# Retention queries and keys of a four-branch decoder trunk: projected and rotated feature-major, with only the keys transposed

## The chip, the cores and the metric

The kernel runs on one core of one Trainium2 chip. The metric is the device time of one execution in microseconds; a kernel's time is the median of its runs.

## What is computed

A trunk of two layers on 1024 tokens of width 1024. Each layer normalises its input, modulates it, and projects it through one input matrix to the inputs of four mixing branches (HGRN2, retention, Mamba-2 SSD, GLA). The branch outputs are normed per head, gated and projected back. The change concerns the retention branch, four heads of width 128:

```python
def rotary(t):
    ...
    t1, t2 = tf[..., : d // 2], tf[..., d // 2:]
    return jnp.concatenate([t1 * cos - t2 * sin, t1 * sin + t2 * cos], axis=-1)

def retention_branch(q_in, k_in, v_in, g_in, onorm_g):
    q = rotary(to_heads(q_in, RET_HEADS))
    k = rotary(to_heads(k_in, RET_HEADS)) * (dk ** -0.5)
    ...
    o = chunked_scalar_decay(q, k, to_heads(v_in, RET_HEADS), log_a)
    return group_rmsnorm(from_heads(o), onorm_g, RET_HEADS) * jax.nn.silu(g_in)
```

The chunked sum is, per chunk of 128 tokens here: scores of queries against keys times a decay mask, times the values, plus the queries times a carried state; the state takes up decayed keys times values.

## The kernel before

**Operands.** All large matmuls run in fp32r with both operands split into a high part (a cast) and a low part (the rest), as three matmuls: high by high, high by low, low by high. The normalised input lies feature-major in SBUF (`hh`, `hl`: 8 k-tiles of 128 features by 1024 tokens, in two halves of 512 tokens). Weights come in slices of 128 x 512 on SP's queue (`raw`, two buffers); ScalarE casts the high part (L405) and VectorE subtracts for the low part (L406), into four buffers each.

**Two forms of the input projection.** `proj_f` (L424) makes 128 output features for all 1024 tokens: the weights stand still in the array and 512 tokens pass, 16 steps of three matmuls of 512 columns (L420 to L422), results feature-major in two PSUM banks. `proj_t` (L453) makes 256 output features for all tokens: 128 tokens stand still and 256 weight columns pass, 64 steps of three matmuls of 256 columns (L467, L469, L470), results token-major in four PSUM banks. All projections share a pool of four banks (`pp`). Both call an `evac` function as each bank is finished.

**The order of work.** The order on TensorE is the order in which the program is written, and it is interleaved by hand. A mixing function is a generator that yields the nanoseconds of other work wanted at that point. `run` hands them to `fill`, which takes steps from a queue of projection generators, each step with a price of its own: 640 for a `proj_f` step or for half an output unit (three matmuls of 512 columns), 320 for a `proj_t` step. `drain(p)` takes the rest of the queue up to generator p. On the other engines and the DMA queues a scheduler orders the instructions, and each queue runs in order.

**The retention stage.** While the second SSD group is mixed (`ssd_mix`, L1029), the queue holds an output projection, then `ret_qk` for head 0 (L865) and `vg_proj` for its values and gates. While head h is mixed (`ret_mix`, L890) the queue holds `ret_qk` and `vg_proj` for head h + 1, for head 0 behind the output projection of tiles 10 and 11. For head 3 it holds the output projection of tiles 4 and 5 (16 units of two steps), then that of tiles 6 and 7 (`out_tiles`, L1173), whose weights are loaded, multiplied by the gate on GpSimd (L1148) and split when it starts.

`ret_qk` projects query and key of one head together with `proj_t`. For each bank (two token tiles) ScalarE copies queries and keys to SBUF (L877), VectorE makes four products per query and key with the cosine and sine tables (L881 to L884), and GpSimd subtracts and adds them (L885, L886). `ret_mix` then transposes eight query and eight key tiles on TensorE (L897), copies them out on ScalarE (L898), scales the token-major keys by the decay to the chunk's end on VectorE (L900), yields 1200, makes the scores (L910) and their mask product (L912), and goes through `scan` (L652): scores by values (L661), keys by values (L667, into bank `ms`), queries by state (L671), the state update (L677), and the head norm with its gate (`head_norm_gate`: squares L541 on ScalarE, rsqrt L272 and L274 on GpSimd, the product L545 on VectorE). The normed output is transposed (L524) some steps later.

Large tiles of 128 x 1024 (tables, queries, keys, values, gates and others) share eleven buffers, tiles of 128 x 512 five. In the SSD mix TensorE writes each chunk's output to bank `po` (L1102), which VectorE reads (L1117, L1120).

Of the kernel before, what the change touches and what calls it, by code (L numbers as in the profile page):

```python
# [16 lines left out]
AF = mybir.ActivationFunctionType  # L17
ALU = mybir.AluOpType
MUL, ADD, SUB = ALU.mult, ALU.add, ALU.subtract
PSUM = bass.MemoryType.PSUM  # L20

P = 128
# [3 lines left out]
NT = L // P  # L26
DEPTH = 2
EPS = 1e-6
C = 128
NC = L // C  # L30
# [5 lines left out]
RQ, RK, RV, RG = 2048, 2560, 3072, 3584  # L36
# [9 lines left out]
def _f(name, col):  # L46
    F_UNITS[name] = len(F_COLS)
    F_COLS.append(col)


def _t(name, c0, c1):
    T_UNITS[name] = len(T_COLS)
    T_COLS.append((c0, c1))
# [15 lines left out]
    _f(("mc", _g), MX + 768 + 128 * _g)  # L69
    _t(("mz", _g), MZ + 256 * _g, MZ + 256 * _g + 128)  # L70
for _h in range(4):
    _t(("rqk", _h), RQ + 128 * _h, RK + 128 * _h)
    _t(("rvg", _h), RV + 128 * _h, RG + 128 * _h)


# [38 lines left out]
CST, NCST = {}, 0  # L114
# [16 lines left out]
def shape_constants():  # L131
    i = np.arange(P)
    out = np.zeros((P, NCST), np.float64)

    def put(name, a):
        o, n = CST[name]
        out[:, o : o + n] = np.asarray(a).reshape(P, n)

    put("ident", np.eye(P))
    put("upper", i[:, None] <= i[None, :])  # L140
    put("ones", np.ones((P, P)))
    log_gamma = np.log1p(-np.exp2(-(5.0 + np.arange(4))))
    dk = 128.0 ** -0.5
    causal = (i[:, None] <= i[None, :]).astype(np.float64)
    grow = np.exp(-log_gamma[None, :] * (i[:, None] + 1))
    put("rmask", causal[:, None, :] * grow[:, :, None] * dk)
    put("rke", np.exp(log_gamma[None, :] * (C - 1 - i[:, None])) * dk)
    put("reps", EPS * grow * grow)
    inv_freq = (10000.0 ** (-np.arange(0, 128, 2, dtype=np.float32) / np.float32(128))).astype(np.float32)
    ang = np.arange(L, dtype=np.float32)[:, None] * inv_freq[None, :]  # L150
    ang = ang.reshape(NT, P, 64).transpose(1, 0, 2).astype(np.float64)
    rot = np.stack([np.cos(ang), np.sin(ang)], axis=1).reshape(P, 2 * NT * 64)
    return out.astype(np.float32), rot.astype(np.float32), [float(np.exp(g * C)) for g in log_gamma]


# [11 lines left out]
def hybrid_trunk(ctx, nc, tc, t_in, out, gamma_c):  # L167
    vec, act, gp, pe = nc.vector, nc.scalar, nc.gpsimd, nc.tensor
# [14 lines left out]
    def nm(s):  # L183
        seq[0] += 1
        return f"{s}_{seq[0]}"

    def big_t():
        return big.tile([P, 1024], F32, tag="b4", name=nm("b4"))

    def mid_t(n=512):  # L190
        return mid.tile([P, 512], F32, tag="b2", name=nm("b2"))[:, :n]
# [4 lines left out]
    def ps_proj():  # L196
        return pp.tile([P, 512], F32, tag="pp", name=nm("pp"))

    def ps_mix(tag, bufs=1):
        return pm.tile([P, 512], F32, tag=tag, bufs=bufs, name=nm(tag))  # L200
# [34 lines left out]
    cs = cst.tile([P, NCST], F32, name="cs")  # L235
# [5 lines left out]
    def k_(name, sub=None):  # L241
        o, n = CST[name]
        return cs[:, o : o + n]
# [5 lines left out]
    ident, upper, ones = k_("ident"), k_("upper"), k_("ones")  # L249
# [27 lines left out]
    def bc(ap, shape):  # L277
        return ap.to_broadcast(shape)
# [145 lines left out]
    def proj_f(l, name, evac):  # L424

        pss = [ps_proj(), ps_proj()]
        for k in range(KT):
            if k % 4 == 0:
                w = load_f(l, name, k // 4)
            for half in range(2):  # L430
                step_f(w, pss[half], half, k)
                if k == KT - 1:
                    evac(half, pss[half])
                yield 640
# [18 lines left out]
    def proj_t(l, name, evac):  # L453

        src = t_in["wt"][l, T_UNITS[name]]
        pss = [ps_proj() for _ in range(4)]
        for s in range(4):
            raw = raw_t(512)
            nc.sync.dma_start(raw, src[:, s * 512 : (s + 1) * 512])
            hi, lo = split(raw, 512)  # L460
            for k in (2 * s, 2 * s + 1):
                j = (k % 2) * 256
                for m in range(NT):
                    o = pss[m // 2][:, (m % 2) * 256 : (m % 2) * 256 + 256]
                    hhi = hh[m // 4][:, k, (m % 4) * P : (m % 4) * P + P]
                    hlo = hl[m // 4][:, k, (m % 4) * P : (m % 4) * P + P]
                    pe.matmul(o, hhi, hi[:, j : j + 256], start=(k == 0 and m % 2 == 0), stop=False,  # L467
                              skip_group_check=True)
                    pe.matmul(o, hhi, lo[:, j : j + 256], start=False, stop=False, skip_group_check=True)  # L469
                    pe.matmul(o, hlo, hi[:, j : j + 256], start=False, stop=(k == KT - 1), skip_group_check=True)  # L470
                    if k == KT - 1 and m % 2:
                        evac(m // 2, pss[m // 2].rearrange("p (m c) -> p m c", m=2))
                    yield 320
# [255 lines left out]
    def vg_tiles():  # L729
        return (big_t().rearrange("p (m c) -> p m c", m=NT), big_t().rearrange("p (m c) -> p m c", m=NT))  # L730
# [127 lines left out]


    def ret_tables():  # L860
        rt = big_t()
        nc.sync.dma_start(rt, t_in["rot"])
        return (rt[:, 0:512].rearrange("p (m d) -> p m d", m=NT), rt[:, 512:1024].rearrange("p (m d) -> p m d", m=NT))

    def ret_qk(l, h, tables, u):  # L865
        if not tables:
            tables.extend(ret_tables())
        cos, sin = tables

        def ev(j, ps):  # L870
            if j == 0:
                u["q"], u["k"] = vg_tiles()
            ms_ = slice(2 * j, 2 * j + 2)
            c2 = cos[:, ms_, :]
            s2 = sin[:, ms_, :]
            for qk, o in (("q", 0), ("k", 128)):
                act.copy(u[qk][:, ms_, :], ps[:, :, o : o + 128])  # L877
            for qk in ("q", "k"):
                x1, x2 = u[qk][:, ms_, 0:64], u[qk][:, ms_, 64:128]
                t = mid_t().rearrange("p (i m d) -> p i m d", i=4, m=2)  # L880
                vec.tensor_tensor(t[:, 0], x1, c2, MUL)  # L881
                vec.tensor_tensor(t[:, 1], x2, s2, MUL)
                vec.tensor_tensor(t[:, 2], x1, s2, MUL)
                vec.tensor_tensor(t[:, 3], x2, c2, MUL)  # L884
                gp.tensor_tensor(u[qk][:, ms_, 0:64], t[:, 0], t[:, 1], SUB)  # L885
                gp.tensor_tensor(u[qk][:, ms_, 64:128], t[:, 2], t[:, 3], ADD)  # L886

        yield from proj_t(l, ("rqk", h), ev)

    def ret_mix(l, h, u, between=None):  # L890
        AT = ATs[h % 2]
        QT, KTt = big_t(), big_t()
        for half in range(2):
            for src, dst, tag in ((u["q"], QT, "sc"), (u["k"], KTt, ("ms", "po")[half])):
                ps = ps_mix(tag, 2 if tag == "sc" else 1)
                for i in range(4):
                    pe.transpose(ps[:, i * P : (i + 1) * P], src[:, half * 4 + i, :], ident)  # L897
                act.copy(dst[:, half * 512 : half * 512 + 512], ps)  # L898
        o, _ = CST["rke"]
        vec.tensor_scalar(u["k"], u["k"], cs[:, o + h : o + h + 1], None, MUL)  # L900
        ke = u["k"]
        o, _ = CST["rmask"]
        rm = cs[:, o + h * P : o + (h + 1) * P]
        oe, _ = CST["reps"]
        yield 1200
        for half in range(2):
            ps = ps_mix("sc", 2)
            for i in range(4):
                c = half * 4 + i
                pe.matmul(ps[:, i * P : (i + 1) * P], KTt[:, c * C : (c + 1) * C], QT[:, c * C : (c + 1) * C],  # L910
                          start=True, stop=True)
            vec.tensor_tensor(AT[:, half * 4 : half * 4 + 4, :], ps.rearrange("p (c t) -> p c t", c=4),  # L912
                              bc(rm.unsqueeze(1), [P, 4, P]), MUL)
            yield 200
        yield 600
        yield from scan(l, 4 + h, AT, lambda c: QT[:, c * C : (c + 1) * C], lambda c: ke[:, c, :], u["v"], u["g"],
                        lambda c: gamma_c[h], cs[:, oe + h : oe + h + 1], h >= 2, between)
# [324 lines left out]
    u, w0, acc, known = {}, {}, {}, [0, 0]  # L1242
# [75 lines left out]
    for l in range(DEPTH):  # L1318
# [5 lines left out]
        p = add(wide)  # L1324
# [7 lines left out]
        for h in range(4):  # L1332
# [7 lines left out]
            if h < 3:  # L1340
                p = add(hgrn_proj(l, h + 1, nu))
            else:
                p = add(gla_qk(l, 0, nu))
# [12 lines left out]
            u = nu  # L1356
# [8 lines left out]
        for p in range(2):  # L1365
# [16 lines left out]
            u = nu  # L1382
# [4 lines left out]
        for g in range(2):  # L1387
# [4 lines left out]
            if g == 0:  # L1392
                add_out(l, (14, 15))
                p = add(ssd_bc(l, 1, nu))
            else:
# [3 lines left out]
                p = add(vg_proj(l, ("rvg", 0), nu))  # L1399
            run(ssd_mix(l, g, u, st, lambda: more_x(nu) if g == 0 else None))  # L1400
            drain(p)
            u = nu
        for h in range(3):
# [4 lines left out]
            p = add(vg_proj(l, ("rvg", h + 1), nu))  # L1408
            run(ret_mix(l, h, u))
            drain(p)  # L1410
            u = nu
# [19 lines left out]
        if more:  # L1431
            u = {}
# [69 lines left out]
```

## Time and profile before

| what | value |
|---|---|
| median of three runs | 2083.54 us (2083.15 to 2085.19) |
| the profiled execution | 2084.53 us |
| its span, first to last instruction | 2082.7 us |
| TensorE clock granted, mean | 0.993 |
| matmuls | 17994 |
| DMA, mean | 60 GB/s |

The page gives the busy time of each engine (PE is TensorE, PEld its weight loads, DVE VectorE, ACT ScalarE, POOL GpSimd, SP the queue that issues most loads), then the span in slices, the chain of work that ended last, and the costliest groups of instructions: line, engine and operation, output and inputs by the program's names, shape, count, busy time, mean nanoseconds of one, and the idle time just before them with what ended it. Matmuls are pipelined, and their ends in the records are modelled. A row of a timeline has the start in us, the busy time, and the instruction. A row of waits has who waited for whom, the us in total, the times, and the longest. A row of a table by windows has the stretch, then the busy time and count on PE, PEld, DVE, ACT and POOL, the granted clock, and the DMA share and GB/s.

### The profile page before, as it was taken

How to read it: one execution, taken by the hardware profiler on the slowest of the kernel's cores; microseconds unless marked ns; L12 is line 12 of the kernel's file. 1: busy time of each engine (PE TensorE's matmuls, PEld its weight loads, DVE VectorE, ACT ScalarE, POOL GpSimd, SP SyncE). 2: the span in 40 equal slices, each digit the busy share in tenths (PEclk: the TensorE clock that was granted, in tenths of full speed). 3: DMA queues.
4: the chain of work that ended last, by engine and by line, in shares of the span. 5: the costliest groups of instructions: out<-in, count | busy, mean ns of one | idle time of the engine just before them, and what ended most of it. 6: DMA issues, size and time to landing. Idle time of an engine off the chain costs nothing.

```text
span 2082.7 us, 42807 instructions
## 1 busy us (share of the span) xinstructions
PE 2030.5 (97%) x17994; PEld 1822.1 (87%) x17994; DVE 1167.2 (56%) x2347; ACT 757.9 (36%) x1760; POOL 382.6 (18%) x564
## 2 busy tenths in 40 slices
PE   5999999999999999999999999999999999999997
PEld 4898888789888899999879888888988989999996
DVE  7656743836537476444555555356464565744456
ACT  7432223432345343122273223343234444322223
POOL 4101001000123233222220010010101323402232
PEclk9999999999999999999999999999999999999999
DMA  8233321111121120111112211111111212111112
GB/s 283 88 104 97 98 77 32 35 39 37 36 66 57 44 89 26 52 37 31 46 54 71 79 32 42 39 35 38 37 40 37 80 43 72 56 37 42 42 36 101
DMA packets 72304, 124.15 MB, mean 60 GB/s; under 512 B 10128, under 2 KB 20656, under 8 KB 72112
## 3 DMA queue, kind: packets, MB, share of 16 engines
q1 hardware_dynamic: 67216, 112.31, 17.6%
q10 hardware_dynamic: 4896, 9.12, 1.4%
q8 instruction: 141, 2.31, 0.5%
q14 instruction: 51, 0.42, 0.1%
HBM read 117.14 MB, written 4.26 MB: 58 GB/s over the span
## 4 chain that ended last, share of the span: by engine, by line
PE 85%; DVE 7%; ACT 4%; DMA 2%; issue 1%; POOL 1%; SPq 0%; POOLq 0%; ACTq 0%; DVEq 0%
PE pp L1159 14%; PE pp L467 12%; PE pp L469 11%; PE pp L470 11%; PE pp L420 7%; PE pp L422 6%; PE pp L421 6%; DMA wa<-in_w_ada 2%; PE sc L584 2%; PE sc L524 1%; DVE b L612 1%; PE po L1102 1%; PE ms L667 1%; PE pp L502 1%; DVE b L301 1%
## 5 line engine op out<-in xcount | busy, mean ns | idle before, releaser
L467 PE MATMUL pp<-whi,hh 128*128 128x256 f32 x2176 | 631.6, 290 | 0.7 <-ACT b L991 0.7
L469 PE MATMUL pp<-wlo,hh 128*128 128x256 f32 x2176 | 615.9, 283 | 0.0
L470 PE MATMUL pp<-whi,hl 128*128 128x256 f32 x2176 | 615.9, 283 | 0.0
L467 PEld LDWEIGHTS pp<-whi,hh 128*128 128x128 f32 x2176 | 417.2, 192 | 4.7 <-ACT b L991 1.5
L469 PEld LDWEIGHTS pp<-wlo,hh 128*128 128x128 f32 x2176 | 417.6, 192 | 0.5
L470 PEld LDWEIGHTS pp<-whi,hl 128*128 128x128 f32 x2176 | 417.1, 192 | 0.0
L405 ACT CAST whi<-raw 128x512 fp32r<-128x512 f32 x280 | 173.6, 623 | 593.9 <-PE pp L470 296.3
L406 DVE TENSOR_TENSOR wlo<-raw,whi 128x512 fp32r<-128x512 f32 x276 | 200.1, 729 | 282.2 <-ACT whi L405 275.2
L420 PE MATMUL pp<-hh,whi 128*128 128x512 f32 x640 | 268.2, 419 | 7.4 <-ACT hh L397 6.6
L422 PE MATMUL pp<-hl,whi 128*128 128x512 f32 x640 | 252.6, 395 | 1.4 <-DVE hl L398 1.3
L421 PE MATMUL pp<-hh,wlo 128*128 128x512 f32 x640 | 251.0, 392 | 0.0
L1164 DVE TENSOR_TENSOR xs<-xs,pp 128x512 f32<-128x512 f32 x256 | 172.9, 684 | 70.8 <-PE pp L1159 68.1
L1159 PE MATMUL pp<-whi,yh 128*128 128x512 f32 x448 | 188.4, 420 | 0.0
L1148 POOL TENSOR_TENSOR raw<-raw,gate_b 128x512 f32<-128x512 f32 x64 | 84.6, 1325 | 521.2 <-DMA raw<-in_w_out 407.3
L1159 PE MATMUL pp<-whi,yl 128*128 128x512 f32 x448 | 175.5, 392 | 0.0
L1159 PE MATMUL pp<-wlo,yh 128*128 128x512 f32 x448 | 174.9, 390 | 0.0
L420 PEld LDWEIGHTS pp<-hh,whi 128*128 128x128 f32 x640 | 120.9, 189 | 32.9 <-ACT hh L397 8.6
L422 PEld LDWEIGHTS pp<-hl,whi 128*128 128x128 f32 x640 | 120.6, 188 | 32.3 <-DVE hl L398 5.5
L421 PEld LDWEIGHTS pp<-hh,wlo 128*128 128x128 f32 x640 | 121.3, 190 | 20.1 <-DVE wlo L406 0.4
L272 POOL TENSOR_SCALAR rt<-ss 128x4 f32<-128x4 f32 (+1 forms) x46 | 12.2, 265 | 556.6 <-ACT junk L541 498.2
L301 DVE SCALAR_TENSOR_TENSOR b<-wa,c_act,b 128x512 f32<-128x512 f32 x84 | 71.2, 847 | 61.7 <-DMA wa<-in_w_ada 60.9
L1159 PEld LDWEIGHTS pp<-whi,yh 128*128 128x128 f32 x448 | 84.4, 188 | 21.1 <-issue 3.4
(257 smaller groups left out, 3075.4 us busy)
## 6 DMA issues: line engine op xcount, KB each, us to landing
raw<-in_wt SPq DMA_DIRECT2D x136, 256.0 KB, 3.0
wa<-in_w_ada SPq DMA_DIRECT2D x96, 256.0 KB, 2.9
raw<-in_wf SPq DMA_DIRECT2D x80, 256.0 KB, 2.6
raw<-in_w_out SPq DMA_DIRECT2D x64, 256.0 KB, 2.6
b<-cum ACTq DMA_DIRECT2D x32, 256.0 KB, 3.5
xs<-in_x SPq DMA_DIRECT2D x8, 512.0 KB, 8.1
out<-b SPq DMA_DIRECT2D x7, 512.0 KB, 2.6
b<-in_wt SPq DMA_DIRECT2D x4, 384.0 KB, 4.1
```

The source lines that it names most:

```text
L301: vec.scalar_tensor_tensor(acc, w, c_act[:, k : k + 1], acc, MUL, ADD)
L405: act.copy(hi, raw)
L406: eng.tensor_tensor(lo, raw, hi.bitcast(F32), SUB)
L420: pe.matmul(ps, hi[:, j : j + P], hh[half][:, k, :], start=(k == 0), stop=False)
L421: pe.matmul(ps, lo[:, j : j + P], hh[half][:, k, :], start=False, stop=False)
L422: pe.matmul(ps, hi[:, j : j + P], hl[half][:, k, :], start=False, stop=(k == KT - 1))
L467: pe.matmul(o, hhi, hi[:, j : j + 256], start=(k == 0 and m % 2 == 0), stop=False, skip_group_check=True)
L469: pe.matmul(o, hhi, lo[:, j : j + 256], start=False, stop=False, skip_group_check=True)
L470: pe.matmul(o, hlo, hi[:, j : j + 256], start=False, stop=(k == KT - 1), skip_group_check=True)
L1148: gp.tensor_tensor(raw, raw, gate_b[:, nh * 512 : (nh + 1) * 512], MUL)
L1159: pe.matmul(ps, a[:, o : o + P], b, start=(n == 0), stop=(n == 3 * len(kts) - 1))
L1164: vec.tensor_tensor(xv, xv, ps, ADD)
```

## The change

The units `rqk` of `proj_t` are replaced by two units of `proj_f` a head, one for the queries and one for the keys. The two tables are laid out feature-major, 128 x 1024 each, the sine with its sign. Of each finished bank ScalarE copies the two halves of 64 features crosswise to SBUF, VectorE multiplies the bank by the cosine, and GpSimd multiplies the crossed copy by the sine and adds it. The mix uses queries and keys as they come; it transposes only the keys, and ScalarE applies the scale of the keys while it copies them out. The `yield 1200` behind the transposes is gone.

```diff
 for _h in range(4):
-    _t(("rqk", _h), RQ + 128 * _h, RK + 128 * _h)
+    _f(("rq", _h), RQ + 128 * _h)
+    _f(("rk", _h), RK + 128 * _h)
     _t(("rvg", _h), RV + 128 * _h, RG + 128 * _h)
...
-    ang = ang.reshape(NT, P, 64).transpose(1, 0, 2).astype(np.float64)
-    rot = np.stack([np.cos(ang), np.sin(ang)], axis=1).reshape(P, 2 * NT * 64)
+    ang = ang.T.astype(np.float64)
+    cos, sin = np.cos(ang), np.sin(ang)
+    rot = np.stack([np.concatenate([cos, cos]), np.concatenate([-sin, sin])])
...
     def ret_tables():
-        rt = big_t()
-        nc.sync.dma_start(rt, t_in["rot"])
-        return (rt[:, 0:512].rearrange("p (m d) -> p m d", m=NT), rt[:, 512:1024].rearrange("p (m d) -> p m d", m=NT))
+        rt = [big_t(), big_t()]
+        for i in range(2):
+            nc.sync.dma_start(rt[i], t_in["rot"][i])
+        return rt
...
-        def ev(j, ps):
-            if j == 0:
-                u["q"], u["k"] = vg_tiles()
-            ms_ = slice(2 * j, 2 * j + 2)
-            c2 = cos[:, ms_, :]
-            s2 = sin[:, ms_, :]
-            for qk, o in (("q", 0), ("k", 128)):
-                act.copy(u[qk][:, ms_, :], ps[:, :, o : o + 128])
-            for qk in ("q", "k"):
-                x1, x2 = u[qk][:, ms_, 0:64], u[qk][:, ms_, 64:128]
-                t = mid_t().rearrange("p (i m d) -> p i m d", i=4, m=2)
-                vec.tensor_tensor(t[:, 0], x1, c2, MUL)
-                vec.tensor_tensor(t[:, 1], x2, s2, MUL)
-                vec.tensor_tensor(t[:, 2], x1, s2, MUL)
-                vec.tensor_tensor(t[:, 3], x2, c2, MUL)
-                gp.tensor_tensor(u[qk][:, ms_, 0:64], t[:, 0], t[:, 1], SUB)
-                gp.tensor_tensor(u[qk][:, ms_, 64:128], t[:, 2], t[:, 3], ADD)
-
-        yield from proj_t(l, ("rqk", h), ev)
+        def ev(name):
+            def ev_(half, ps):
+                if half == 0:
+                    u[name] = big_t()
+                s = slice(half * 512, half * 512 + 512)
+                t = mid_t()
+                act.copy(t[0:64, :], ps[64:P, :])
+                act.copy(t[64:P, :], ps[0:64, :])
+                vec.tensor_tensor(u[name][:, s], ps, cos[:, s], MUL)
+                gp.tensor_tensor(t, t, sin[:, s], MUL)
+                gp.tensor_tensor(u[name][:, s], u[name][:, s], t, ADD)
+            return ev_
+
+        yield from proj_f(l, ("rq", h), ev("q"))
+        yield from proj_f(l, ("rk", h), ev("k"))
...
-        QT, KTt = big_t(), big_t()
+        QT, KTt = u["q"], u["k"]
+        o, _ = CST["rke"]
+        ke = big_t().rearrange("p (c d) -> p c d", c=NC)
         for half in range(2):
-            for src, dst, tag in ((u["q"], QT, "sc"), (u["k"], KTt, ("ms", "po")[half])):
-                ps = ps_mix(tag, 2 if tag == "sc" else 1)
-                for i in range(4):
-                    pe.transpose(ps[:, i * P : (i + 1) * P], src[:, half * 4 + i, :], ident)
-                act.copy(dst[:, half * 512 : half * 512 + 512], ps)
-        o, _ = CST["rke"]
-        vec.tensor_scalar(u["k"], u["k"], cs[:, o + h : o + h + 1], None, MUL)
-        ke = u["k"]
+            ps = ps_mix(("ms", "po")[half])
+            for i in range(4):
+                c = half * 4 + i
+                pe.transpose(ps[:, i * P : (i + 1) * P], KTt[:, c * C : (c + 1) * C], ident)
+            act.activation(ke[:, half * 4 : half * 4 + 4, :], ps.rearrange("p (c d) -> p c d", c=4), AF.Copy,
+                           scale=cs[:, o + h : o + h + 1])
...
-        yield 1200
```

## The prediction

> **What bounds the kernel now.** I read the page's busy table and granted clock first, then the chain that ended last.
>
> ```profile
> span 2082.7 us, 42807 instructions
> PE 2030.5 (97%) x17994; PEld 1822.1 (87%) x17994; DVE 1167.2 (56%) x2347; ACT 757.9 (36%) x1760; POOL 382.6 (18%) x564
> PE 85%; DVE 7%; ACT 4%; DMA 2%; issue 1%; POOL 1%; SPq 0%; POOLq 0%; ACTq 0%; DVEq 0%
> L467 PE MATMUL pp<-whi,hh 128*128 128x256 f32 x2176 | 631.6, 290 | 0.7 <-ACT b L991 0.7
> ```
>
> TensorE carries the kernel: what leaves its instruction stream leaves the time, as long as the other engines stay ahead of it. The column "mean ns of one" is a trap here: matmuls overlap, so 290 ns is a life, not a spacing. The price of a matmul is the distance between starts, and that is in the timeline of TensorE. First a stretch of a token-major projection, then one of a feature-major projection:
>
> ```profile
> 719.72 0.28 PE L470 MATMUL pp<-whi,hl 128*128 128x256 f32 x1
> ...
> 725.84 0.28 PE L470 MATMUL pp<-whi,hl 128*128 128x256 f32 x1
> ```
>
> ```profile
> 647.83 0.40 PE L420 MATMUL pp<-hh,whi 128*128 128x512 f32 x1
> ...
> 651.93 0.39 PE L420 MATMUL pp<-hh,whi 128*128 128x512 f32 x1
> ```
>
> Between the first two rows stand 51 starts: 6.12 / 51 = 0.120 us for 256 columns. Between the other two stand 18: 4.10 / 18 = 0.228 us for 512. Two matmuls of 256 columns cost 0.240, one of 512 costs 0.228: some 12 ns go per matmul, whatever its width.
>
> **Projection.** A head's query and key columns are now 64 steps of 3 matmuls of 256 columns (192 x 0.120 = 23.04 us); they become two units of 16 steps of 3 matmuls of 512 (96 x 0.2278 = 21.87 us). That is 1.17 us a head, and with 4 heads in 2 layers 9.4 us. Weights are still four slices of 512 columns a head, so casts, low parts and loads stay in number. By the page "TensorE: Matmul & The Clock Gate" of the Trainium skill (section Back-to-back issue gap) 256 and 512 columns take 262 and 518 cycles at 2.4 GHz, 109.2 and 215.8 ns; by that, an estimate, this term would be 0.24 us a head, 2 us in all; the starts above are 11 to 12 ns wider each, and they decide.
>
> **Transposes.** The mix loses the eight query transposes of each head.
>
> ```profile
> 813.52 0.60 PE L897 MATMUL sc<-cs,b 128*128 128x128 f32 x4
> ...
> 815.19 0.47 PE L1159 MATMUL pp<-whi,yh 128*128 128x512 f32 x1
> ```
>
> Sixteen stand between the two starts, 1.67 us: 0.104 each. Eight are 0.84 us; over 8 heads 6.7 us. Nothing covers either term, TensorE being the bound.
>
> **The other engines.** These are the groups of instructions that go, and those nearest to what comes:
>
> ```profile
> L877 ACT COPY b<-pp 128x256 f32<-128x256 f32 x64 | 20.7, 376 | 22.9 <-PE pp L470 21.6
> L898 ACT COPY b<-sc 128x512 f32<-128x512 f32 x16 | 9.5, 596 | 0.0
> L881 DVE TENSOR_TENSOR b<-b,b 128x128 f32<-128x128 f32 x64 | 19.6, 305 | 20.2 <-ACT b L877 18.1 <-POOL b L886 2.0
> L882 DVE TENSOR_TENSOR b<-b,b 128x128 f32<-128x128 f32 x64 | 30.0, 468 | 0.0
> L883 DVE TENSOR_TENSOR b<-b,b 128x128 f32<-128x128 f32 x64 | 28.8, 450 | 0.0
> L884 DVE TENSOR_TENSOR b<-b,b 128x128 f32<-128x128 f32 x64 | 18.4, 288 | 0.0
> L900 DVE TENSOR_SCALAR b<-b,cs 128x1024 f32<-128x1024 f32 x8 | 6.0, 753 | 5.1 <-PE po L897 5.1
> L885 POOL TENSOR_TENSOR b<-b 128x128 f32<-128x128 f32 x64 | 44.1, 689 | 90.0 <-DVE b L883 89.2 <-ACT b L877 0.6 <-ACT whi L405 0.3
> L886 POOL TENSOR_TENSOR b<-b 128x128 f32<-128x128 f32 x64 | 34.5, 540 | 0.0
> L799 ACT COPY b<-pp 64x512 f32<-64x512 f32 x8 | 4.7, 583 | 0.1
> L532 ACT ACTIVATE yh<-sc,cols 128x512 fp32r<-128x512 f32 x56 | 38.6, 689 | 92.1 <-PE sc L524 91.6
> L1164 DVE TENSOR_TENSOR xs<-xs,pp 128x512 f32<-128x512 f32 x256 | 172.9, 684 | 70.8 <-PE pp L1159 68.1
> L1148 POOL TENSOR_TENSOR raw<-raw,gate_b 128x512 f32<-128x512 f32 x64 | 84.6, 1325 | 521.2 <-DMA raw<-in_w_out 407.3 <-ACT b L650 59.2 <-DVE b L737 17.8
> ```
>
> Per head (a group's count over 8): VectorE loses 8 x (0.305 + 0.468 + 0.450 + 0.288) + 0.75 = 12.8 us and gets four products out of PSUM, at L1164's price 2.7 us. ScalarE goes from 8 x 0.376 + 4 x 0.596 = 5.4 to 8 x 0.583 + 2 x 0.689 = 6.0. GpSimd goes from 8 x (0.689 + 0.540) = 9.8 to 8 x 1.325 = 10.6. None is near the 45 us that TensorE spends on a head's two projections, so these matter only by what they delay. The price of a cross-half copy is not shown (L799 stays on its partitions): between 0.38 (L877) and 0.60 (L898), 0.583 taken. A second table adds one load on SP's queue per layer:
>
> ```profile
> L862 SPq DMA_DIRECT2D b<-in_rot x2: 377/382/388, 729.9 to 1746.8; - x2
> ```
>
> It is issued at 729.9, more than 50 us ahead of the rotation products that read it (784.41 below); behind it on SP are the query's weight slices, which go out one issue (0.38 us) later. The eleven large buffers balance: in the mix 2 tables + 4 + 4 + 1 where there were 1 + 4 + 4 + 2. If the second table had to wait for a buffer, the weight queue behind it would wait too; 0 to 3 us, taken as 0.
>
> **Waits that go.** TensorE's waits, from the view of who waited for whom:
>
> ```profile
> PE pp L1159 <- DVE wlo L406: 3.7, 2, 1.9
> PE po L1102 <- DVE s L1120: 1.5, 2, 0.8
> PE sc L524 <- DVE b L1138: 0.5, 1, 0.5
> ```
>
> The L1102 wait stands once a layer at the end of head 0's rotation, and VectorE's timeline shows why:
>
> ```profile
> 784.41 0.54 DVE L882 TENSOR_TENSOR b<-b,b 128x128 f32<-128x128 f32 x1
> ...
> 788.89 0.41 DVE L1120 TENSOR_TENSOR s<-po,dx 128x256 f32<-128x256 f32 x1
> ```
>
> The SSD chunk's reads of `po` are queued behind rows of rotation products. With four products a head instead of 32 they go first; the L524 wait hangs on the same queue. Gain 0 to 2.0 us, 2.0 taken.
>
> The L406 wait is in the tail of each layer:
>
> ```profile
> 1032.76 1.02 POOL ry L274
> ...
> 1033.80 1.13 DVE b L545 x4
> ...
> 1035.52 0.62 DVE wlo L406
> ...
> 1036.18 6.47 PE pp L1159 x20
> ```
>
> ```profile
> 1036.00:1042.00 6.00, 5.82 (x18) 4.63 (x19) 2.71 (x6) 1.15 (x2) 0.00 (x0) 0.72 0.26 87
> ```
>
> Head 3's last norm (squares, rsqrt, L545) stands on VectorE ahead of the low parts of the last output weights. The removed `yield 1200` is two filler steps: the output projection of tiles 4 and 5 has 32, of which 30 ran before that norm and 28 now will. So TensorE has 2 x 3 x 0.228 = 1.37 us more to do behind the norm, and the 1.9 us wait falls to about 0.5: 1.4 us in layer 0. There the clock row shows 0.72 over the next 6 us, 6 x 0.28 = 1.7 us lost after the wait; whether 0.5 us of waiting still sets that off no row says, and I count no. In layer 1 I count half of the 1.4, since the final norms follow. Sum 3.8, bounds 0 and 4.8.
>
> **A wait that comes.** The keys' two banks must be empty when the value projection, which takes all four, comes round. The nearest case is a decay projection of the HGRN stage:
>
> ```profile
> 1294.41 0.60 ACT L707 ACTIVATE b<-pp 128x512 f32<-128x512 f32 x1 [2.74 <-PE pp L422]
> ...
> 1294.90 0.28 PE L467 MATMUL pp<-whi,hh 128*128 128x256 f32 x1
> ```
>
> ```profile
> 811.56 0.42 DVE L737 COPY b<-pp 128x256 f32<-128x256 f32 x1 [2.20 <-PE pp L470]
> 812.02 0.39 ACT L738 ACTIVATE b<-pp 128x256 f32<-128x256 f32 x1 [2.08 <-DVE b L737]
> ```
>
> The second pair shows that two engines read one bank one after the other. The last bank is wanted after six steps of 0.36, at 1294.90 + 2.16 = 1297.06. Four copies of 0.583 from 1294.41 end at 1296.74, VectorE's product of 0.684 at 1297.43, with hand-overs 0.5 us late. Eight heads: 4.0 us. Below: 0, if the copies overlap. Above: a cast (0.6) and a low part (0.7) queued ahead, 1.8 each, 14.4.
>
> **Sum.** 9.4 + 6.7 + 2.0 + 3.8 - 4.0 = 17.9 us. The profiled execution took 2084.53 us (span 2082.7), 1.0 above the median of the three timed runs, 2083.54; taken from the median: 2065.6.
>
> **Rivals.** First, the bank wait is dearer: at 1.8 us a head, with no gain in the tail or at L1102, 9.4 + 6.7 - 14.4 = 1.7 remain, 2081.8. For it: eight hand-overs straight on TensorE's path. Against: casts run slices ahead, and in the HGRN case nothing waited.
>
> Second, slower: GpSimd. In heads 1 and 2 the mix runs over the next head's query projection. Counted in filler steps of 0.683 us, the first query product can reach GpSimd at step 17, the second half's rsqrt at step 22, and the transposes that need it come at 33. Four rotation instructions of d us stand ahead; the rsqrt then waits 4d - 3.4. From rsqrt to L545's end are 2.2 us in the tail's rows (1032.76 to 1034.93), some 2.5 with the small instruction ahead, of the 7.5 in the 11 steps, so TensorE waits 4d - 8.4 in each of 4 mixes, and may lose 1.7 of clock. It decides from 4 x (4d - 8.4 + 1.7) = 17.9, d = 2.8 us, twice L1148's. A GpSimd row beside VectorE's dense products, four times L885's mean, shows that such stretching exists:
>
> ```profile
> 790.79 2.80 POOL L885 TENSOR_TENSOR b<-b 128x128 f32<-128x128 f32 x1 [1.67 <-DVE b L883]
> ```
>
> At d = 4.0 it gives 4 x 9.3 - 17.9 = 19.3 us more than before, 2102.8. Against it: those dense products are what the change removes. The GPSIMD Engine Reference of the Trainium skill (section Specifications) says that GpSimd shares its SBUF interfaces with VectorE and contends with instructions of two SBUF inputs; the rows agree, and by that rule the new product, with one input in PSUM, would press less.
>
> Third, only columns count: if 512 columns cost twice 0.120, the projection term is 0, 2075.0; the starts speak against it. The rule of the Trainium skill cited under the projection comes near to this case. Fourth, the lives are the price: 192 x 0.28 against 96 x 0.39, 16.3 us a head, 1945; the overlap speaks against it. Fifth, the tail and L1102 gains come and no bank waits: 22 us or more, 2061 and below.
>
> **Numbers.** Forecast 0.64 (2061 to 2071); dear bank wait 0.17 (0.09 still faster by over 0.2%, 0.06 within, 0.02 slower); GpSimd 0.06; columns 0.03; lives 0.01; more gain 0.09. 0.2%, 4.2 us, is about what a measurement can tell. The range runs from 2057 to 2078: the upper end takes in a bank wait of 1.5 us a head with half of the other gains.
>
> **What would show it.** Right: 832 fewer matmuls; feature-major starts 0.228 apart at the rotation's weights; 64 fewer transposes; no L1102 wait at the end of head 0; a shorter wait in layer 0's tail and a full clock behind it; a wait of about 0.5 us at the start of each value projection of the retention. Wrong: GpSimd products over 2.8 us with transposes of the normed output waiting, or waits over 2 us on a bank.

## The result, and the profile after

| | before | changed |
|---|---|---|
| median | 2083.35 us (2082.24 to 2085.19) | 2062.44 us (2061.59 to 2065.35) |
| the profiled execution | 2084.53 us | 2062.73 us |
| its span | 2082.7 us | 2060.9 us |

The ratio of the times is 0.9901, with an interval of 0.9884 to 0.9918: 21 us faster, where 17.9 had been worked out. In a later comparison the changed kernel took 2062.47 us, ratio 0.9905 (0.9888 to 0.9921).

The page of the changed kernel: span, busy table, shares of the chain that ended last, and the group of token-major projection matmuls.

```profile
span 2060.9 us, 40807 instructions
PE 2012.4 (98%) x17162; PEld 1771.7 (86%) x17162; DVE 1114.3 (54%) x2115; ACT 769.7 (37%) x1744; POOL 398.6 (19%) x500
PE 87%; DVE 5%; ACT 4%; DMA 2%; issue 1%; POOL 0%; POOLq 0%; SPq 0%; ACTq 0%; DVEq 0%
L469 PE MATMUL pp<-whi,hh 128*128 128x256 f32 x1664 | 480.6, 289 | 1.2 <-ACT b L990 0.7
```

There are 832 fewer matmuls (17994 to 17162): 96 per head from the projection and 8 from the transposes, times eight. TensorE is as full as it was, so its instruction stream still sets the time. Lines have moved by one or two: L406 is L408 now, L524 is L526, L545 is L547, L1159 is L1158, L1164 is L1163.

The feature-major steps of a query or key unit, in TensorE's timeline of the changed kernel (28 starts between the two rows):

```profile
849.52 0.39 PE L423 MATMUL pp<-hh,wlo 128*128 128x512 f32 x1
...
855.87 0.39 PE L424 MATMUL pp<-hl,whi 128*128 128x512 f32 x1
```

6.35 / 28 = 0.2268 us from start to start, as counted on. The rotation's instructions, in the view that groups one line's instructions (count, then least, median and longest duration in ns, first and last start, shape):

```profile
L880 ACT COPY b<-pp x32: 582/585/587, 766.1 to 1976.1; 64x512 f32<-64x512 f32 x32
L882 DVE TENSOR_TENSOR b<-pp,b x32: 691/692/693, 767.3 to 1977.3; 128x512 f32<-128x512 f32 x32
L883 POOL TENSOR_TENSOR b<-b,b x32: 1287/1296/1757, 767.3 to 1980.5; 128x512 f32<-128x512 f32 x32
L884 POOL TENSOR_TENSOR b<-b,b x32: 1267/1292/1710, 768.7 to 1981.8; 128x512 f32<-128x512 f32 x32
```

The crossed copies at 0.585 and the product at 0.692 came at the prices taken (0.583 and 0.684). GpSimd's instructions have a median of 1.29 and a longest of 1.76, against the 2.8 from which the slower rival would have decided; the longest row of the rotation before was 2.80.

In the view of who waited for whom, the L1102 and L524 waits of before are gone, and the tail's wait has halved:

```profile
PE pp L1158 <- DVE wlo L408: 2.2, 2, 1.1
```

TensorE's timeline is so regular between waits that a stage's length repeats within 0.1 us from kernel to kernel. That makes a table of stages the sharpest view of this case. Each column is the distance, in us, between two starts in TensorE's timeline: the first matmul of the second SSD mix, the first score matmul of each retention head, the last transpose of the next layer's norm (layer 0) or the last matmul (layer 1), and for the last column the end of the last instruction.

| kernel | SSD to head 0, layer 0 / 1 | head 0 to 1 | 1 to 2 | 2 to 3 | head 3 to the layer's end, 0 / 1 | last matmul to end |
|---|---|---|---|---|---|---|
| before | 89.82 / 88.87 | 77.49 | 55.31 | 55.27 | 81.71 / 52.01 | 10.03 |
| changed | 84.57 / 84.57 | 75.98 | 53.78 | 53.79 | 80.65 / 52.59 | 8.49 |
| 256 columns | 86.98 / 86.92 | 77.08 | 54.65 | 54.65 | 80.62 / 52.58 | 8.49 |
| dead transposes | 85.44 / 85.44 | 76.99 | 54.85 | 54.86 | 80.79 / 52.69 | 8.50 |
| yield back | 85.95 / 85.95 | 76.03 | 53.83 | 53.80 | 80.06 / 53.63 | 10.04 |
| one copy empties the bank | 85.91 / 86.00 | 75.37 | 53.54 | 53.55 | 80.66 / 52.59 | 8.50 |
| GpSimd's sum thrice | 92.03 / 91.18 | 75.98 | 55.13 | 55.10 | 80.70 / 52.67 | 8.49 |
| sum on VectorE | 84.67 / 84.57 | 76.00 | 53.73 | 53.75 | 80.68 / 52.63 | 8.51 |
| shorter tail yield | 84.57 / 84.57 | 76.00 | 53.78 | 53.80 | 79.34 / 51.22 | 10.35 |
| both edits | 84.57 / 84.57 | 75.38 | 53.54 | 53.55 | 79.33 / 51.22 | 10.33 |
| both, tail in layer 0 only | 84.57 / 84.57 | 75.37 | 53.54 | 53.55 | 79.27 / 52.59 | 8.50 |

(Layer 1's head-to-head distances are within 0.03 of layer 0's.) The retention stages give 10.8 us in layer 0 (5.25 + 1.51 + 1.53 + 1.48 + 1.06), 8.2 in layer 1, and 1.5 at the end, 20.6 of the 21.8 us of the two spans. The rest lies in stages that the change does not touch, and their length differs from profile to profile. From layer 0's end to the second SSD mix of layer 1 it is 657.3 us before, 658.1 in the changed kernel and 657.3 in the changed kernel's second profile. The clock is full there in all three; the changed kernel has one wait that the kernel before has not, and its second profile has it at 0.6 us:

```profile
PE sc L603 <- DVE b L614: 1.2, 1, 1.2
```

Ahead of layer 0's second SSD mix (726.84 us before, 724.82 changed) it is also stretches in the clock column of the table by windows that move, such as this one of before, against the changed kernel:

```profile
355.00:361.00 6.00, 6.00 (x38) 5.88 (x39) 0.92 (x2) 1.90 (x2) 0.00 (x0) 0.72 0.14 35
```

```profile
355.00:361.00 6.00, 6.00 (x53) 6.00 (x52) 1.54 (x3) 2.50 (x4) 0.00 (x0) 1.00 0.20 52
```

Such a stretch costs 1.7 us (6 x 0.28). None of this is credited to the change.

### The profile page after: what moved, and what is told of

It is laid out like the page before. It is cut to its first block, busy times and chain, and to the rows that moved or that the text cites. A ratio compares the mean times of both kernels' runs of the same rounds, so it can differ in the third digit from the quotient of the medians.

```text
span 2060.9 us, 40807 instructions
## 1 busy us (share of the span) xinstructions
PE 2012.4 (98%) x17162; PEld 1771.7 (86%) x17162; DVE 1114.3 (54%) x2115; ACT 769.7 (37%) x1744; POOL 398.6 (19%) x500
## 3 DMA queue, kind: packets, MB, share of 16 engines
q1 hardware_dynamic: 67504, 113.36, 17.9%
## 4 chain that ended last, share of the span: by engine, by line
PE 87%; DVE 5%; ACT 4%; DMA 2%; issue 1%; POOL 0%; POOLq 0%; SPq 0%; ACTq 0%; DVEq 0%
PE pp L1158 15%; PE pp L422 10%; PE pp L424 10%; PE pp L423 9%; PE pp L469 9%; PE pp L471 9%; PE pp L472 9%; DMA wa<-in_w_ada 2%; PE sc L586 1%; PE sc L526 1%; PE po L1101 1%; DVE b L614 1%; PE ms L669 1%; DVE b L303 1%; PE pp L504 1%
## 5 line engine op out<-in xcount | busy, mean ns | idle before, releaser
L469 PE MATMUL pp<-whi,hh 128*128 128x256 f32 x1664 | 480.6, 289 | 1.2 <-ACT b L990 0.7
L471 PE MATMUL pp<-wlo,hh 128*128 128x256 f32 x1664 | 470.5, 283 | 0.0
L472 PE MATMUL pp<-whi,hl 128*128 128x256 f32 x1664 | 470.5, 283 | 0.0
L422 PE MATMUL pp<-hh,whi 128*128 128x512 f32 x896 | 375.2, 419 | 6.9 <-ACT hh L399 6.1
L408 DVE TENSOR_TENSOR wlo<-raw,whi 128x512 fp32r<-128x512 f32 x276 | 208.5, 757 | 294.6 <-ACT whi L407 287.6
L424 PE MATMUL pp<-hl,whi 128*128 128x512 f32 x896 | 353.4, 394 | 0.8 <-DVE hl L400 0.7
L423 PE MATMUL pp<-hh,wlo 128*128 128x512 f32 x896 | 351.1, 392 | 0.0
L469 PEld LDWEIGHTS pp<-whi,hh 128*128 128x128 f32 x1664 | 318.6, 191 | 6.4 <-DVE b L882 1.6
L471 PEld LDWEIGHTS pp<-wlo,hh 128*128 128x128 f32 x1664 | 318.8, 192 | 0.6
L472 PEld LDWEIGHTS pp<-whi,hl 128*128 128x128 f32 x1664 | 318.6, 191 | 0.0
L1163 DVE TENSOR_TENSOR xs<-xs,pp 128x512 f32<-128x512 f32 x256 | 173.2, 684 | 67.3 <-PE pp L1158 64.5
L423 PEld LDWEIGHTS pp<-hh,wlo 128*128 128x128 f32 x896 | 170.1, 190 | 28.1 <-DVE wlo L408 0.4
L1158 PE MATMUL pp<-whi,yh 128*128 128x512 f32 x448 | 188.0, 420 | 0.0
L1158 PE MATMUL pp<-whi,yl 128*128 128x512 f32 x448 | 175.4, 392 | 0.0
L1158 PE MATMUL pp<-wlo,yh 128*128 128x512 f32 x448 | 174.9, 390 | 0.0
L1158 PEld LDWEIGHTS pp<-whi,yh 128*128 128x128 f32 x448 | 84.4, 188 | 21.2 <-issue 3.4
```

What stands on the lines that cost most here:

```text
L408: eng.tensor_tensor(lo, raw, hi.bitcast(F32), SUB)
L422: pe.matmul(ps, hi[:, j : j + P], hh[half][:, k, :], start=(k == 0), stop=False)
L423: pe.matmul(ps, lo[:, j : j + P], hh[half][:, k, :], start=False, stop=False)
L424: pe.matmul(ps, hi[:, j : j + P], hl[half][:, k, :], start=False, stop=(k == KT - 1))
L1158: pe.matmul(ps, a[:, o : o + P], b, start=(n == 0), stop=(n == 3 * len(kts) - 1))
L1163: vec.tensor_tensor(xv, xv, ps, ADD)
```

## The experiments

All are edits of the changed kernel, each timed against the kernel before on the chip on which it ran itself.

### The projection alone: 256 columns per matmul

```diff
-        yield from proj_f(l, ("rq", h), ev("q"))
-        yield from proj_f(l, ("rk", h), ev("k"))
+        yield from proj_f(l, ("rq", h), ev("q"), 2)
+        yield from proj_f(l, ("rk", h), ev("k"), 2)
```

With the new last argument a step is made as six matmuls of 256 columns instead of three of 512.

> The changed kernel with each matmul of the retention's query and key projections split into two of 256 columns: the same columns in all, 96 more matmuls and weight loads a head. If every matmul pays some 12 ns whatever its width (0.120 us for 256 columns, 0.228 for 512), this gives the projection term back: 96 x 0.2278 becomes 192 x 0.120, +1.17 us a head, +9.4 us, about 2072. If only columns count, the time stays within 2 us of 2062.4. By the skill's figures (109.2 and 215.8 ns) it would be +2 us.

Measured: 2075.23 us, 0.9957 (0.9945 to 0.9969). In its timeline 42 starts take 5.03 us, 0.1198 each:

```profile
851.00 0.28 PE L426 MATMUL pp<-hh,whi 128*128 128x256 f32 x1
...
856.03 0.28 PE L426 MATMUL pp<-hh,whi 128*128 128x256 f32 x1
```

The stages lose 2.4 + 1.1 + 0.9 + 0.9 = 5.2 us a layer (rounded), 10.4 in all; the other 2.2 us by which the profiled span is longer lie in stages that the edit does not touch. Of head 0's 2.4, 1.37 are a new wait for a bank at the start of its value projection, where this kernel stops twice:

```profile
787.01 0.29 PE L480 MATMUL pp<-whi,hl 128*128 128x256 f32 x1
787.92 0.39 PE L477 MATMUL pp<-whi,hh 128*128 128x256 f32 x1 [0.62 <-DVE b L890]
...
788.62 0.28 PE L480 MATMUL pp<-whi,hl 128*128 128x256 f32 x1
789.12 0.39 PE L477 MATMUL pp<-whi,hh 128*128 128x256 f32 x1 [0.22 <-DVE b L890]
```

(0.91 + 0.50 from start to start, less 0.24 for two plain ones, and 0.10 more for each of the two matmuls behind a stop, whose next start comes 0.22 us later and not 0.12.) The price of the width itself is what the matmuls of the query and key projections take, each from its own start to the next: in heads 0 to 3 they go from 22.52 to 23.55, 22.03 to 23.18, 23.26 to 24.11 and 23.27 to 24.11 us, so 1.03, 1.15, 0.85 and 0.84 us a head, 7.7 us over both layers. The case that only columns count, which gives 0, falls. So does the 0.24 us a head by the cycle counts of the Trainium skill (TensorE: Matmul & The Clock Gate, section Back-to-back issue gap), which that section gives for a matmul by itself, not for a stream with a weight load for each, as here.

### The query transposes put back as dead work

```diff
+            spare_ps = ps_mix("sc", 2)
+            for i in range(4):
+                c = half * 4 + i
+                pe.transpose(spare_ps[:, i * P : (i + 1) * P], QT[:, c * C : (c + 1) * C], ident)
+            act.copy(seen, spare_ps[:, 0:1])
```

> The changed kernel with the eight query transposes of each head put back on TensorE as dead work (into a free bank, one column read by ScalarE, result unused). If transposes cost their spacing on a full TensorE: 64 x 0.104 to 0.109, +6.7 to +7.0 us, about 2069. If such short matmuls run in the shadow of others: no change, 2062 to 2063.

Measured: 2071.38 us, 0.994 (0.9928 to 0.9952). Head 0 loses 0.87 us, the others 1.01 to 1.07. Between the transposes' rows there is no gap, and before the scores there is a small one:

```profile
885.36 0.60 PE L905 MATMUL sc<-cs,b 128*128 128x128 f32 x4
885.79 0.60 PE L899 MATMUL po<-cs,b 128*128 128x128 f32 x4
886.23 0.60 PE L905 MATMUL sc<-cs,b 128*128 128x128 f32 x4
886.75 1.16 PE L915 MATMUL sc<-b,b 128*128 128x128 f32 x8
```

Four transposes take 0.435 us, so eight take 0.87 and the term is 7.0 us. The 0.52 before the score row holds some 0.1 more, and in heads 1 to 3 the score matmuls take another 0.1; both are the experiment's own, since the changed kernel has neither. That they come from the bank that the small copy has to read is likely and not shown.

### The yield put back

```diff
         oe, _ = CST["reps"]
+        yield 1200
         for half in range(2):
```

> The changed kernel with the yield of 1200 back behind the transposes. If the tail's gain comes from two filler steps that moved behind the last norm, the gap between output matmuls in each layer's tail goes from 1.50 back to 2.26 us, +0.8 us a layer, and a stretch of half clock may follow (+1.7): +1.5 to +3.3 us, 2064 to 2066, nothing else moving. If the wait in the tail hangs on something else (the scale on ScalarE, the sum on GpSimd): no change in the tail, 2062.4.

Measured: 2069.10 us, 0.9928 (0.9916 to 0.994), dearer than expected; of the 8.0 us by which the profiled span is longer, 3.1 lie in stages that the edit does not touch. The wait of before is back whole:

```profile
PE pp L1159 <- DVE wlo L408: 3.7, 2, 1.9
```

Two filler steps move ahead of the scores (+1.38 in the first column, the same less in the sixth), and behind that shift the tail loses 0.79 us a layer (80.06 + 1.38 - 80.65). In layer 1 1.7 us more follow at half clock, seen in the table by windows:

```profile
2037.00:2043.00 6.00, 6.00 (x21) 4.68 (x20) 3.74 (x6) 1.15 (x2) 0.81 (x2) 0.72 0.00 0
```

In before that stretch stood in layer 0 and not in layer 1. So of four waits of this length (2.26 us from start to start), two were followed by half clock, while of the waits of 1.5 us in the changed kernel's tails none was. And the end grew by 1.55 us, to the length of before. In the changed kernel the chain that ended last is TensorE's up to its last matmul, then one output add and the last norm:

```profile
2044.91 7.95 PE pp L1158 x35
...
2052.88 0.70 DVE xs L1163
```

With the yield back, it leaves TensorE at 2051.13 and goes through four output adds (L1164) with the final norms between them:

```profile
2051.13 0.70 DVE xs L1164
...
2054.73 1.28 DVE b L1200
2056.01 0.61 DVE xs L1164
...
2060.05 0.69 DVE xs L1164
2060.76 0.69 DVE b L1225
2061.46 0.60 DVE xs L1164
```

This is the gain that the prediction had not seen. Why the yield brings the norms onto the chain was not followed further.

### The bank emptied by one copy

```diff
-                act.copy(t[0:64, :], ps[64:P, :])
-                act.copy(t[64:P, :], ps[0:64, :])
-                vec.tensor_tensor(u[name][:, s], ps, cos[:, s], MUL)
+                act.copy(u[name][:, s], ps)
+                act.copy(t[0:64, :], u[name][64:P, s])
+                act.copy(t[64:P, :], u[name][0:64, s])
+                vec.tensor_tensor(u[name][:, s], u[name][:, s], cos[:, s], MUL)
```

In the changed kernel the keys' second bank is released by VectorE's product, behind four copies. In head 1 the sequence is the one of the prediction: the copies on ScalarE, the product on VectorE, and TensorE, which wants the bank at 863.15 (0.12 us after its start at 863.03).

```profile
860.37 0.58 ACT L880 COPY b<-pp 64x512 f32<-64x512 f32 x1 [4.13 <-PE pp L424]
...
862.17 0.58 ACT L881 COPY b<-pp 64x512 f32<-64x512 f32 x1
```

```profile
862.78 0.69 DVE L882 TENSOR_TENSOR b<-pp,b 128x512 f32<-128x512 f32 x1 [0.51 <-ACT b L881]
```

```profile
863.03 0.28 PE L472 MATMUL pp<-whi,hl 128*128 128x256 f32 x1
863.52 0.39 PE L469 MATMUL pp<-whi,hh 128*128 128x256 f32 x1 [0.22 <-DVE b L882]
```

> The changed kernel with each bank emptied by one ScalarE copy, and the crossed copies and VectorE's product made from that copy: the bank is held 0.6 us and not 1.9, ScalarE gets 0.6 us more a bank. If the gaps of 0.50, 0.27 and 0.27 us in the value projections of heads 1, 2 and 3 are the keys' banks, they go: about 0.4 to 0.6 us less in head 1 and 0.25 in heads 2 and 3, in both layers -1.5 to -2.5 us, 2060 to 2061. If they have another cause they stay, and ScalarE's extra copies leave 2062 to 2064.

Measured: 2064.55 us, 0.9909 (0.9897 to 0.9922), not faster. Heads 1 to 3 gain 0.61, 0.24 and 0.24 us per layer, as expected, which prices the bank wait of the changed kernel at 2.2 us in all. But head 0 loses 1.34 and 1.43. ScalarE's queue in order shows why:

```profile
785.43 0.42 ACT L1130 ACTIVATE junk<-b 128x256 bf16<-128x256 f32 x1 [2.62 <-DVE b L1127]
785.75 0.19 ACT L1130 ACTIVATION_READ_ACCUMULATOR junk<-b 128x1 f32 x1
785.95 0.62 ACT L881 COPY b<-b 64x512 f32<-64x512 f32 x1
786.58 0.62 ACT L882 COPY b<-b 64x512 f32<-64x512 f32 x1
787.22 0.59 ACT L880 COPY b<-pp 128x512 f32<-128x512 f32 x1
```

The copy that would free the second bank stands behind the first bank's crossed copies, and these behind an SSD square that waited 2.62 us for VectorE. TensorE's next matmul started 1.06 us after the one before it, at 787.86; that and the slow start behind it are 1.04 of the 1.34, and the other 0.3 are lost at the SSD mix's matmuls into bank `po` just before (L1102). "One instruction instead of three on the bank" is worth nothing where that one is queued behind a wait.

### GpSimd's sum made three times

```diff
-                gp.tensor_tensor(u[name][:, s], u[name][:, s], t, ADD)
+                for op in (ADD, SUB, ADD):
+                    gp.tensor_tensor(u[name][:, s], u[name][:, s], t, op)
```

This doubles GpSimd's time in the rotation, from 2.6 to 5.2 us a bank.

> The changed kernel with the rotation's sum on GpSimd made three times over (added, subtracted, added): four GpSimd instructions a bank where there were two, 5.3 us more per query or key. By the slower rival's sum the rsqrt of heads 1 and 2 now waits behind 10.6 us and TensorE waits 4 x 10.6 / 4 - 8.4 = 2.2 us in each of four mixes, with 1.7 of half clock each at worst: +9 to +16 us, 2071 to 2078. If the scheduler places the rsqrt between, or the cover is larger than worked out, the heads' spacing stays and the time is 2062 to 2064.

Measured: 2082.61 us, 0.9996 (0.9987 to 1.0005): the whole gain is gone. Two places pay. In heads 1 and 2 the transposes of the normed output wait, as the slower rival had it, for 1.35 and 1.31 us per layer. Head 0 pays more, 7.5 us in layer 0 and 6.6 in layer 1. TensorE's waits from 720 to 1050 us:

```profile
PE po L1102 <- DVE s L1120: 4.3, 1, 4.3
PE sc L526 <- DVE b L547: 1.9, 2, 1.0
```

How GpSimd delays the SSD mix is read from GpSimd's and ScalarE's rows, and was not tried by a run of its own:

```profile
770.97 6.86 POOL L885 TENSOR_TENSOR b<-b,b 128x512 f32<-128x512 f32 x5
```

```profile
777.86 0.33 ACTq L1047 DMA_DIRECT2D b<-cum  x1
778.23 0.99 ACT L1053 ACTIVATE b<-b,cum 128x128 f32<-128x128 f32 x3 [8.96 <-DMA b<-cum]
```

The crossed copy lies in one of the five tiles of 128 x 512, and GpSimd's last sum frees it. The SSD mix loads its decay factors into the same five, from ScalarE's queue. The first load goes out at 774.95; the second is the row at 777.86, 0.03 us after GpSimd's rows end at 777.83. ScalarE, whose queue runs in order, did nothing else in the 8.96 us. In the changed kernel the same two loads go out 0.03 us after the sums that end at 770.00 and 773.04:

```profile
768.71 1.29 POOL L884 TENSOR_TENSOR b<-b,b 128x512 f32<-128x512 f32 x1
...
771.77 1.27 POOL L884 TENSOR_TENSOR b<-b,b 128x512 f32<-128x512 f32 x1
```

```profile
770.03 0.33 ACTq L1046 DMA_DIRECT2D b<-cum  x1
...
773.07 0.33 ACTq L1046 DMA_DIRECT2D b<-cum  x1
```

So the dependence is there in the changed kernel too, with slack. After TensorE's stop in the doubled kernel (4.6 us from start to start) the clock is low, 0.50 over six microseconds:

```profile
786.00:792.00 6.00, 5.58 (x22) 5.25 (x23) 4.29 (x11) 2.86 (x6) 4.54 (x7) 0.50 0.13 42
```

### The rotation's sine product and sum on VectorE

```diff
-                gp.tensor_tensor(t, t, sin[:, s], MUL)
-                gp.tensor_tensor(u[name][:, s], u[name][:, s], t, ADD)
+                vec.tensor_tensor(t, t, sin[:, s], MUL)
+                vec.tensor_tensor(u[name][:, s], u[name][:, s], t, ADD)
```

> The changed kernel with the sine product and the sum on VectorE. If GpSimd's share lies wholly beside other work, nothing is gained by a faster engine; and if VectorE's queue is what held bank po at the end of head 0, the keys' two banks, now some 4.1 us of VectorE's time in a row, bring a wait of 0 to 1 us back there (0.8 before) and make the value projections' waits longer by 0.3 to 0.7 us a head, since the product on a bank stands behind the sum of the bank before: 2063 to 2069. If GpSimd's latency costs time on the path: 2060 or less.

Measured: 2063.66 us, 0.9907 (0.9893 to 0.992). No retention stage differs from the changed kernel's by more than 0.1 us. VectorE makes each at 0.68 us where GpSimd takes 1.29; neither place is on the path.

### A shorter yield ahead of head 3's norm

```diff
-                yield 7000
+                yield 5000
                 to_feature_major(l, y[0], kt, 0, apart)
                 between()
```

> The changed kernel with the wait of head 3's first normed half cut from 7000 to 5000, so that three more filler steps (2.05 us) stand behind its last norm. If the wait in the tail is VectorE's queue behind that norm, the gap of 1.50 us goes to the usual 0.23 in both layers: -1.3 us a layer, -1.3 to -2.6 in all, 2060 to 2061. If the first half's transposes now come too early they wait instead, and nothing is gained.

Measured: 2063.46 us, 0.9908 (0.9894 to 0.9921), no faster than the changed kernel, against the 2060 to 2061 expected. The tail gains 1.3 us in layer 0 and 1.4 in layer 1, and the end loses 1.9: in the last layer this edit costs 0.5.

### Both edits together

The one-copy bank for heads 1 to 3 only, and the shorter yield.

> The changed kernel with the shorter wait of the run before and, in heads 1 to 3 alone, the banks emptied by one copy; head 0, where the extra copies made TensorE wait 1.4 us, as in the change. The bank part showed -0.61, -0.24 and -0.24 us a layer at heads 1 to 3, so -2.2 us; with the tail's -1.3 to -2.6: 2058 to 2059. If the two interfere (the copies of head 3 in the tail's queue): 2060 to 2062.

Measured: 2061.17 us, 0.9892 (0.9877 to 0.9907). The stages of both edits come as they did alone, so the two do not interfere; the end, at 10.33 us as with the shorter yield alone, takes 1.9 back. Then the shorter yield in layer 0 alone:

```diff
-                yield 5000
+                yield 5000 if l + 1 < DEPTH else 7000
```

> The keys' and queries' banks of heads 1 to 3 emptied by one copy, and the shorter yield ahead of the norm of head 3 in the first layer alone; the last layer's tail is that of the changed kernel. Theory: the bank edit gives 0.61 + 0.24 + 0.24 = 1.1 us per layer, 2.2 in all; the tail gives 1.4 in layer 0; and since layer 1 keeps its yield, the end from the last matmul to the last instruction stays at 8.5 us. Sum 3.6 us less than the changed kernel, about 2059 beside 2062.5. Rival: the length of the end hangs not on that yield but on something that differs by kernel or by execution; then it may come out near 10.3 us here too, and about 2060.5. A half-clock stretch in the first projections of a layer can add 1.5 to either.

Measured: 2060.59 us, 0.9897 (0.9882 to 0.9912). No wait for low parts is left in layer 0's tail, and the end is 8.50 us again. The median lies where the rival had it (2060.5), but the end of the profile does not, and the end is what the rival was about. Beside it on the same chip the changed kernel once more:

> The changed kernel once more, on the same chip: within 0.1% of its first median, 2062.4, with the end from the last matmul at 8.5 us by the theory that it belongs to the yield, and between 8.5 and 10.3 by the rival. Half-clock stretches in the early projections of a layer, if they come by execution and not by kernel, may stand at other places than in its first profile.

Measured: 2062.47 us, 0.9905 (0.9888 to 0.9921), the end at 8.50. So the end's length belongs to the yields of the last layer: of the kernels above, the three that move them to either side have 10.0 to 10.4, and all that keep them as changed have 8.5. In the profiles the best version's stages are 3.6 us shorter (2 x 1.1 + 1.4); its median is 1.9 lower, and the intervals of the two overlap, so that this last gain is read from the stages and not proven by the times.

## Why the prediction held, step by step

| term | worked out | measured | from |
|---|---|---|---|
| projection | 9.4 | 7.7 | 256 columns |
| transposes | 6.7 | 7.0 | dead transposes |
| L1102 and L524 waits | 2.0 | 3.0 | what is left of the first column |
| tail, both layers | 3.8 | 3.2 | yield back |
| end of the kernel | none | 1.5 | yield back |
| bank wait | -4.0 | -2.2 | one copy |
| sum | 17.9 | 20.2 | |

The 20.2 stand beside 20.6 us by the stages and 21 by the medians. The forecast's 17.9 is 2.3 less: the bank wait was taken 1.8 too high and the end (1.5) not at all, and the other misses, -1.7 to +1.0, add up to -1.0. The tail's 3.2 are 0.79 in each layer and 1.65 of lost clock in layer 0. The third row is a remainder: 5.25 in layer 0 less 1.38 of shift by the yield, 0.87 and 1.03 leaves 1.97; 4.30 in layer 1 leaves 1.02. The view of waits before has 1.3 and 0.8 for them. That VectorE's 32 products a head caused it was argued from the profile and not tried alone; the sum on VectorE shows that eight more instructions a head do not bring it back.

**Projection.** The step was right: the distance between starts is the price. It came out at 1.03 and 1.15 us in heads 0 and 1 and 0.85 and 0.84 in heads 2 and 3. In head 2, 14 of the 96 matmuls stand right behind a row of the mix, and there one of 512 columns takes 0.315 us to the next start and two of 256 take 0.201 + 0.120, so that halving costs next to nothing; the other 82 are 0.230 apart and not 0.228, against 0.120 as before. Why they are wider stays open.

**Transposes, VectorE's queue, prices on ScalarE and GpSimd.** As worked out, but for the 0.104 us of a transpose: the row that closed the prediction's stretch started 0.03 us behind the last transpose, while the transposes themselves are 0.109 apart. ScalarE and GpSimd were not on the path, which the sum on VectorE shows for GpSimd.

**The tail.** The step "the 1.9 us wait falls to about 0.5" was mis-sized: it fell to 1.1 in both layers. TensorE had two more filler steps to do, but these finish an output unit earlier, and so VectorE has two output adds ahead of the low part, not one. Its rows in the changed kernel:

```profile
1022.01 1.13 DVE L547 SCALAR_TENSOR_TENSOR b<-sc,ry,b 128x128 f32<-128x128 f32 x4 [1.74 <-POOL ry L276]
1023.06 1.28 DVE L1163 TENSOR_TENSOR xs<-xs,pp 128x512 f32<-128x512 f32 x2
1024.25 1.29 DVE L408 TENSOR_TENSOR wlo<-raw,whi 128x512 fp32r<-128x512 f32 x2
```

Of the 1.37 us moved, one add took 0.6. The lost clock of layer 0, which was counted as 1.7, did go: the windows behind the wait show 1.00. Since such a stretch followed only two of the four waits of the old length, these 1.7 us belong to the profiled execution of before and not surely to every one.

```profile
1025.00:1031.00 6.00, 6.00 (x28) 5.00 (x29) 3.86 (x6) 1.84 (x3) 0.00 (x0) 1.00 0.29 87
```

The half credit for layer 1's wait, "since the final norms follow", was no bad guess for the wait (0.8 of it came) and missed the end: there 1.5 us more came.

**The bank wait.** The working, half a microsecond a head, holds in head 1 alone (0.61). In heads 2 and 3 four transposes of the normed output (0.35 us) stand in TensorE's stream behind the first value step, so the bank is wanted that much later, and in head 0 no wait shows. The term was taken eight times from one head's geometry.

**The slower rival.** Its mechanism is real and its place was wrong. At doubled GpSimd work it costs 1.3 us in each of heads 1 and 2, where its formula, with eight GpSimd instructions ahead instead of four, gives 8 x 1.325 - 8.4 = 2.2 before any lost clock. The dear place is head 0, through the shared tiles and ScalarE's queue, which the prediction had not looked at. Its threshold (d of 2.8 us, where 1.29 was measured) fits the doubled kernel, which lost the whole gain, by luck alone: of the 19.4 us that the stages lost, only 5.3 came in its place.

## What to carry to other kernels

Where TensorE bounds and its matmuls come evenly, price an edit by distances between starts, and read the result as a table of stages: their lengths repeat to 0.1 us and separate terms that the total time, with its stretches of lost clock, mixes. Before moving work to an idle engine, ask not only who waits for its result but what its operands occupy: here a tile freed late by GpSimd holds up a load on ScalarE, and with it a mix that has nothing to do with the rotation. A wait that is priced for one head must be placed anew in each, since the work interleaved around it differs.

## What the runs showed of the hardware

A half-clock stretch of about 3.4 us (1.7 us lost) followed two of four TensorE stops of 2.26 us and none of the changed kernel's stops of 1.5 us; after the stop of 4.6 us the clock was 0.50 over the next six. Stretches that look alike (0.72 over six microseconds at 355 us) stand in some profiles and not in others in stages that are the same in all, so that no rule for them comes out of these runs.

GpSimd's sine product, at a median of 1.296 us in the changed kernel, is slower where VectorE's product beside it reads both inputs from SBUF, as it does in the kernel whose banks are emptied by one copy:

```profile
L884 POOL TENSOR_TENSOR b<-b,b x32: 1290/1746/1809, 769.2 to 1983.8; 128x512 f32<-128x512 f32 x32
```

The medians mix cases, so single rows say it better. In head 2 the sine product at 909.11 of that kernel took 1.73 us with nothing beside it on VectorE but such a product; in the changed kernel the one at 903.06 took 1.29 beside the product that reads the bank, and the one at 973.56 took 1.29 with VectorE idle. The changed kernel's own rows of 1.73 to 1.76 stand beside low parts (L408), which also read two inputs in SBUF. So what tells is whether VectorE reads two inputs from SBUF. That agrees with the rule of the Trainium skill that the prediction cited (GPSIMD Engine Reference, section Specifications), by which GpSimd shares its SBUF interfaces with VectorE and contends with instructions of two SBUF inputs. VectorE pays too: its product, 0.69 us in the changed kernel, took up to 1.70 in the other. No row here reached the 2.80 of the token-major rotation.
